# A hybrid SSD and HGRN2 encoder step: the decays of the SSD chunks computed on GpSimd, a second buffer for one tile, and one norm of the HGRN layer placed a head earlier

## The chip, the cores and the metric

The kernel runs on one core of one Trainium2 chip. The metric is the device time of one execution in microseconds (us). One profiled execution of the kernel before is at hand, with its own time and its trace, beside the times of three other runs.

## The reference, cut to what matters

The program is one inference step of a trunk of two layers, width 1024: a Mamba-2 (SSD) mixer and a SwiGLU feed-forward, then an HGRN2 mixer and another feed-forward, with 1024 prompt frames and 32 sample frames that share all weights. The change touches the scan of the SSD mixer and a norm ahead of the HGRN mixer.

```python
def step(S, inp):                       # one chunk of the SSD scan
    xc, dtc, Bc, Cc = inp
    cum = jnp.cumsum(dtc * Ag, axis=1)
    seg = cum[:, :, None] - cum[:, None, :]
    decay = jnp.where(mask, jnp.exp(jnp.where(mask, seg, 0.0)), 0.0)
    xdt = xc * dtc[..., None]
    cb = jnp.einsum('btgn,bsgn->btsg', Cc, Bc)
    y = jnp.einsum('btsg,btsgh,bsghp->btghp', cb, decay, xdt)
    y = y + jnp.einsum('btgn,bghpn->btghp', Cc, S) * jnp.exp(cum)[..., None]
    last = cum[:, -1]
    w_end = jnp.exp(last[:, None] - cum)
    S = jnp.exp(last)[..., None, None] * S + jnp.einsum('bsgh,bsghp,bsgn->bghpn', w_end, xdt, Bc)
    return S, y

def rmsnorm(x, w):
    xf = x.astype(jnp.float32)
    y = xf * lax.rsqrt(jnp.mean(xf * xf, axis=-1, keepdims=True) + NORM_EPS)
    return (y * w.astype(jnp.float32)).astype(x.dtype)
```

There are 32 SSD heads of 64 in four groups of eight; B and C (128 wide) are shared by a group. Each head has its own running sum `cum`, and so its own matrix of decays in each chunk.

## The kernel before, in words

**Tiling.** The 1056 frames lie along the free axis, in two halves of 512 and 544 columns (the 32 sample frames are the end of the second). A scheduler sorts the instructions of each engine from the order in which the code gives them, from priorities and from the buffers of each kind of tile (`BUFS`, L44); an engine then runs its list in order. Every dense projection is done as three matmuls on parts of the operands (`product`, L307 to 316: L314, L315, L316); for it each weight tile is split by ScalarE (`wh`, through the helper `act`, L98) and VectorE (`wl`, through the helper `tt`, L101). The other helpers are L104 (`stt`, VectorE), L107 (`ts`) and L110 (`dma`, issued on the queue of SyncE, SP). L331 is the matmul with ones that sums squares over the partitions.

**SSD stage.** `ssd_layer` goes through eight units, two halves by four groups. A unit has four chunks of 128 frames, and in the second half a fifth of the 32 sample frames: 36 chunks. Between the steps of a chunk stand projections as fillers for TensorE, among them z (`ssd_z`: ScalarE's tanh of the projection, then VectorE's `z` product).

For a chunk `chunk_loads` (L524) reads the running sums of the group's eight heads from DRAM, spread over all partitions, as two quads (`cumB`, kind `cb`, four buffers, so two chunks), and the factors `ec`. `ssd_chunk` (L543) then does:

- L552, the B C product on TensorE; VectorE multiplies it with the causal mask (`cbm`).
- L557, four transposes of x; VectorE makes `xdt` and `xw` of them.
- the decays: per head one ScalarE clamp of the difference, `relu(col - cumB)` on 128x128; per quad one ScalarE exp on 128x512 with scale −1, and one VectorE product with `cbm`. That is 8, 2 and 2 instructions a chunk.
- L572, the transpose of B, copied out by ScalarE (`Btok`).
- L579, C times the state; L582, the new state's product, from `xw` and `Btok`; L593, the outputs' product, 8 heads, from the products of the decays and `xdt`.

After the chunks of a group `ssd_gate` (L613 on) multiplies the output Y by z, takes its norm (squares on ScalarE, sums on VectorE, L331) and splits it. GpSimd does only small things in all this: it copies three columns at the edges of each tile of the convolution (L488 to L504), and a few powers at the start.

**HGRN stage.** `hgrn_layer` (L860) goes through sixteen units (half, head), with a list of tasks (projections) dealt out among the chunks of each. The norm of the second half is needed from unit (0,7) on. It is the last task of unit (0,6): one call of `norm` with a raised priority, which takes the squares, L331, the root (logarithm and exp on ScalarE, each with a load of its table), and writes eight pieces as a pair of tiles each (`h`, `l`).

`mixed(a, b)` deals the tasks of b evenly among those of a.

Of the kernel before, what the change touches and what calls it, by code (L numbers as in the profile page):

```python
# [11 lines left out]
AF = mybir.ActivationFunctionType  # L12
ALU = mybir.AluOpType
# [9 lines left out]
LEN = (H1, SEQ - H1 + NS)  # L23
# [14 lines left out]
C_SSDN, C_CB, C_FFN, C_HGN, C_GN, C_HG, C_LB = 0, 8, 32, 48, 56, 72, 73  # L38
# [2 lines left out]

TW = 552
FIXED = 14368
BUFS = {"x": 12, "ys": 8, "cb": 4, "xd": 2, "ec": 1, "ss": 1, "xr": 2, "n": 4, "w": 3}  # L44
WIDTH = {k: TW for k in BUFS}


@with_exitstack
def trunk_kernel(ctx, tc, x_prompt, x_sample, state_ssd, cache_conv, state_hgrn,
# [5 lines left out]
    V, A, G, PE = nc.vector, nc.scalar, nc.gpsimd, nc.tensor  # L55
# [17 lines left out]
    def slot(tag, s):  # L73
        return T(tag, s, F32R) if isinstance(tag, str) else tag
# [22 lines left out]
    def act(out, in_, f, **kw):  # L97
        A.activation(out=out, in_=in_, func=f, **kw)  # L98

    def tt(out, a, b, op, eng=None):  # L100
        (eng or V).tensor_tensor(out=out, in0=a, in1=b, op=op)  # L101
# [4 lines left out]
    def ts(out, a, s1, s2, op0, op1, eng=None):  # L106
        (eng or V).tensor_scalar(out=out, in0=a, scalar1=s1, scalar2=s2, op0=op0, op1=op1)  # L107
# [17 lines left out]
    MUL, ADD, SUB = ALU.mult, ALU.add, ALU.subtract  # L125
# [41 lines left out]
    xr = place(9)  # L167
# [170 lines left out]
    XN = [xnt[:, i] for i in range(16)]  # L338
    XN2 = ["x"] * 12 + ["cb"] * 4
# [39 lines left out]
    @lifted("norm")  # L379
    def norm(h, wc, out, tags, blocks=None, r=None):  # L380

        for (b0, bn) in blocks or ((0, LEN[h]),):
            mmb = BLK[h] if blocks is None else [(0, bn)]
            if r is None:
                r = rstd_of([acc[h][m][:, b0:b0 + bn] for m in range(KD)], mmb, 1.0 / D, bn)
            for m in range(KD):
                xf = T("n", "xf")
                stt(xf[:, :bn], acc[h][m][:, b0:b0 + bn], vc[:, wc + m:wc + m + 1], r[:, :bn], MUL, MUL)
                if m == len(out):
                    out.append((slot(tags[2 * m], "h"), slot(tags[2 * m + 1], "l")))  # L390
                xh, xl = out[m]
                act(xh[:, b0:b0 + bn], xf[:, :bn], AF.Copy)
                tt(xl[:, b0:b0 + bn], xf[:, :bn], xh[:, b0:b0 + bn].bitcast(F32), SUB)
        return out
# [8 lines left out]
    st = [place(TW) for _ in range(NG)]  # L403
# [138 lines left out]
    @lifted("chunk")  # L542
    def ssd_chunk(h, g, c, S, loads, u):  # L543
        o, n, smp = CHUNKS[h][c]
        Bt, Ct, xs, Y = u["x"][0], u["x"][1], u["x"][2:], u["Y"]
        cols, elast = dts[h]
        xo = o + (3 if smp else 0)
        Bx, Cx = Bt[:, xo:xo + n], Ct[:, xo:xo + n]
        h0 = g * 8
        cums, ec = loads  # L550
        ps = psum_sc()
        PE.matmul(ps[:n, :n], Bx, Cx, start=True, stop=True)  # L552
        cbm = small("cbm")
        tt(cbm[:n, :n], ps[:n, :n], cmask[:n, :n], MUL)
        ps = psum_sc()
        for j in range(4):
            PE.transpose(ps[:n, j * P:(j + 1) * P], xs[j][:, xo:xo + n], ident)  # L557
        x3 = ps[:n, :].rearrange("p (h q) -> p h q", q=64)
        xdt, xw = T("xd", "xdt")[:, :512], T("xd", "xw")[:, :512]
        tt(xdt[:n, :].rearrange("p (h q) -> p h q", q=64), x3,  # L560
           cols[:n, c, h0:h0 + 8].unsqueeze(2).to_broadcast([n, 8, 64]), MUL)
        tt(xw[:n, :].rearrange("p (h q) -> p h q", q=64), x3,
           cols[:n, c, 64 + h0:64 + h0 + 8].unsqueeze(2).to_broadcast([n, 8, 64]), MUL)
        for q in range(2):
            cb3 = cums[q]
            for i in range(4):
                hh = 32 + h0 + 4 * q + i
                act(cb3[:n, i, :n], cb3[:n, i, :n], AF.Relu, scale=-1.0, bias=cols[:n, c, hh:hh + 1])
            act(cb3[:n, :, :n], cb3[:n, :, :n], AF.Exp, scale=-1.0)
            tt(cb3[:n, :, :n], cb3[:n, :, :n], cbm[:n, :n].unsqueeze(1).to_broadcast([n, 4, n]), MUL)  # L570
        ps = psum_sc()
        PE.transpose(ps[:n, :P], Bx, ident)  # L572
        Btok = small("Btok")
        act(Btok[:n, :], ps[:n, :P], AF.Copy)
        if ec is not None:
            y2 = psum_sc()
            y23 = y2.rearrange("p (j t) -> p j t", t=P)
            for j in range(4):
                PE.matmul(y23[:, j, :n], S[:, j * P:(j + 1) * P], Cx, start=True, stop=True)  # L579
            tt(ec[:, :, :n], y23[:, :, :n], ec[:, :, :n], MUL)  # L580
        pp = psum_sc()
        PE.matmul(pp, Btok[:n, :], xw[:n, :], start=True, stop=True)  # L582
        if ec is None:
            V.tensor_copy(S, pp)
        else:
            S3 = S.rearrange("p (h q) -> p h q", q=64)
            tt(S3, S3, elast[:, h0:h0 + 8, c:c + 1].to_broadcast([P, 8, 64]), MUL)
            tt(S, S, pp, ADD)
        y1 = psum_sc()
        y13 = y1.rearrange("p (j t) -> p j t", t=P)  # L590
        for i in range(8):
            r = 64 * (i % 2)
            PE.matmul(y13[r:r + 64, i // 2, :n], xdt[:n, i * 64:(i + 1) * 64], cums[i // 4][:n, i % 4, :n],  # L593
                      start=True, stop=True)
        yo = Y[:, :, o:o + n]
        if ec is None:
            act(yo, y13[:, :, :n], AF.Copy)
        else:
            tt(yo, y13[:, :, :n], ec[:, :, :n], ADD)
# [260 lines left out]
    def hgrn_layer(after):  # L860
        units = [(h, e) for h in range(2) for e in range(8)]
        us = [{"S": None} for _ in units]
        for f in (hgrn_f, hgrn_q, hgrn_v):
            f(0, 0, us[0])
        for i, (h, e) in enumerate(units):
            u = us[i]
            tasks = [lambda: hgrn_g(h, e, u)]
            if e % 2 == 0 and i:
                ph, pe = units[i - 1]
                tasks += [lambda m4=m4: hgrn_out(ph, pe // 2, m4, [us[i - 2]["y"], us[i - 1]["y"]])  # L870
                          for m4 in range(2)]
            if i + 1 < len(units):
                nh, ne = units[i + 1]
                tasks += [lambda f=f: f(nh, ne, us[i + 1]) for f in (hgrn_f, hgrn_q, hgrn_v)]
            if (h, e) == (0, 6):
                tasks.append(lambda: norm(1, C_HGN, xns[1], XN2))
            if (h, e) == (1, 6):
                tasks += after[:1]
            if (h, e) == (1, 7):
                tasks += after[1:]  # L880
            u["o"] = T("ys", "ho")
            if e % 2 == 0:
                yt = sp.tile([P, 4 * TW], F32R, tag="Y", bufs=1, name=nm("hy"))[:, :4 * LEN[1]]
                yp = yt.rearrange("p (j t) -> p j t", j=4)
            u["yp"] = yp
            nch = len(CHUNKS[h])
            for c in range(nch):
                second = hgrn_chunk(h, e, c, u)
                q = -(-len(tasks) // (nch - c))
                for i2, t in enumerate(tasks[:q]):  # L890
                    if i2 == HB2:
                        second()
                    t()
                if q <= HB2:
                    second()
                tasks = tasks[q:]
            hgrn_gate(h, e, u)
        return [lambda m4=m4: hgrn_out(1, 3, m4, [us[-2]["y"], us[-1]["y"]]) for m4 in range(2)]
# [6 lines left out]
    def x_stat(h, keep):  # L905

        return rstd_of([acc[h][m][:, :LEN[h]] for m in range(KD)], BLK[h], 1.0 / D, LEN[h], keep)

    def norm_pieces(h, wc, out, blocks, r):

        def piece(m, b0, bn):
            xf = T("n", "xf")
            stt(xf[:, :bn], acc[h][m][:, b0:b0 + bn], vc[:, wc + m:wc + m + 1], r[:, b0:b0 + bn], MUL, MUL)
            if m == len(out):
                out.append((XN[2 * m], XN[2 * m + 1]))
            xh, xl = out[m]
            act(xh[:, b0:b0 + bn], xf[:, :bn], AF.Copy)
            tt(xl[:, b0:b0 + bn], xf[:, :bn], xh[:, b0:b0 + bn].bitcast(F32), SUB)
        return [lambda m=m, b=b: piece(m, *b) for b in blocks for m in range(KD)]
# [209 lines left out]
    def mixed(a, b):  # L1129

        out, k = [], 0
        for i, x in enumerate(a):
            out.append(x)
            while k < len(b) and k * len(a) < (i + 1) * len(b):
                out.append(b[k])
                k += 1
        return out + b[k:]
# [163 lines left out]
```

## Time and profile before

| what | before |
|---|---|
| three runs | 2904.81, 2904.77, 2899.86 us, median 2904.77 |
| the profiled execution | 2906.18 us; its span 2904.4 us, mean granted TensorE clock 0.996 |
| idle time of TensorE in the span | 55.6 us |
| instructions in the span | 49072 |
| clamps on ScalarE, exps on ScalarE, products on VectorE | 288, 72 and 72 instructions; 93.4, 42.3 and 44.5 us |

Times in rows are us from the span's start; a timeline row has start, duration, engine, line, operation, the tile written and the tiles read, how many instructions are drawn together, and in brackets the idle time before them with what ended it. A row of groups has the busy time, the mean of one in ns, and the idle time ahead of them. A windows row has the busy time of each engine and its count, then the granted clock of TensorE (1.00 is full), the DMA share and GB/s. A wait for several things is put down to the one that the profile saw last. L98, L101, L104, L107 and L110 are lines of helpers, so operations are told apart by their tiles.

### The profile page before, as it was taken

To read this page: it belongs to the slowest core of one execution; us is meant where nothing else is said; L and a number is where in the kernel's file an instruction comes from. 1 tells how busy PE (TensorE), PEld (TensorE's weight loads), DVE (VectorE), ACT (ScalarE), POOL (GpSimd) and SP (SyncE) were. 2 spreads that over 40 slices of the span, in tenths; PEclk is the share of its full clock that TensorE was granted. 3 is DMA by queue.
4 is the path that set the end of the run, shared out by engine and by line. 5 is a ranking of instruction groups with operands and counts; after the bars stand their busy time and mean duration, and the time that the engine had idled before them with its cause. 6 is when DMAs were issued, how large, how long until landed. Compare 5 with 4: busy or idle time off the path is not lost. (4 is left out here: it accounts for less than half of the span.)

```text
span 2904.4 us, 49072 instructions
## 1 busy us (share of the span) xinstructions
PE 2848.8 (98%) x19711; PEld 2619.9 (90%) x19711; DVE 2152.7 (74%) x3744; ACT 1559.5 (54%) x2922; POOL 46.4 (2%) x156
## 2 busy tenths in 40 slices
PE   8999999999999999999999999999999999999998
PEld 7777788999988999999999888899988999999998
DVE  6777787777787977887777455655568877887777
ACT  6645645554653754456544655655554644554445
POOL 0000000000000000000000000000000000000000
PEclk9999999999999999999999999999999999999999
DMA  5443434344332333323333222222222332333223
GB/s 151 115 111 92 110 82 120 109 114 108 107 90 88 102 111 100 102 80 95 109 95 105 81 82 73 60 79 77 74 84 81 119 100 88 120 94 94 90 88 111
DMA packets 401247, 282.61 MB, mean 97 GB/s; under 512 B 22633, under 2 KB 388730, under 8 KB 401018
## 3 DMA queue, kind: packets, MB, share of 16 engines
q1 hardware_dynamic: 401018, 279.47, 33.2%
q8 instruction: 154, 2.52, 0.3%
q14 instruction: 75, 0.61, 0.1%
HBM read 271.61 MB, written 7.82 MB: 96 GB/s over the span
## 5 line engine op out<-in xcount | busy, mean ns | idle before, releaser
L98 ACT ACTIVATE wh<-raw 128x512 fp32r<-128x512 f32 (+1 forms) x688 | 557.3, 818 | 541.8 <-PE mm L315 419.5
L314 PE MATMUL mm<-xn,wh 128*128 128x272 f32 (+2 forms) x1552 | 524.8, 338 | 0.3 <-ACT wh L98 0.3
L315 PE MATMUL mm<-xn,wh 128*128 128x272 f32 (+2 forms) x1552 | 519.1, 335 | 3.8 <-issue 3.8
L316 PE MATMUL mm<-xn,wl 128*128 128x272 f32 (+2 forms) x1552 | 518.5, 334 | 3.2 <-DVE wl L101 3.2
L101 DVE TENSOR_TENSOR wl<-raw,wh 128x1024 fp32r<-128x1024 f32 x308 | 375.9, 1222 | 83.7 <-ACT wh L98 63.5
L101 DVE TENSOR_TENSOR fixed<-mm,fixed 128x272 f32<-128x272 f32 (+1 forms) x512 | 262.9, 525 | 192.7 <-PE mm L316 191.1
L314 PE MATMUL mm<-fh,wh 128*128 128x272 f32 (+1 forms) x1056 | 341.7, 325 | 1.1 <-DVE fixed L101 0.8
L315 PE MATMUL mm<-fl,wh 128*128 128x272 f32 (+1 forms) x1056 | 341.9, 324 | 0.7 <-DVE fl L101 0.7
L316 PE MATMUL mm<-fh,wl 128*128 128x272 f32 (+1 forms) x1056 | 341.7, 324 | 0.0
L316 PEld LDWEIGHTS mm<-xn,wl 128*128 128x128 f32 x1552 | 293.0, 189 | 37.3 <-issue 6.0
L314 PEld LDWEIGHTS mm<-xn,wh 128*128 128x128 f32 x1552 | 293.0, 189 | 29.5 <-issue 2.6
L315 PEld LDWEIGHTS mm<-xn,wh 128*128 128x128 f32 x1552 | 293.0, 189 | 27.1 <-issue 0.8
L101 DVE TENSOR_TENSOR wh<-raw,wh 128x512 fp32r<-128x512 f32 x380 | 257.1, 688 | 38.5 <-ACT wh L98 35.2
L989 PE MATMUL mm<-th,wh 128*128 128x272 f32 (+1 forms) x912 | 260.4, 286 | 0.1
L990 PE MATMUL mm<-tl,wh 128*128 128x272 f32 (+1 forms) x912 | 259.7, 285 | 0.0
L991 PE MATMUL mm<-th,wh 128*128 128x272 f32 (+1 forms) x912 | 259.6, 285 | 0.0
L314 PEld LDWEIGHTS mm<-fh,wh 128*128 128x128 f32 x1056 | 198.4, 188 | 17.4 <-DVE fixed L101 1.7
L315 PEld LDWEIGHTS mm<-fl,wh 128*128 128x128 f32 x1056 | 198.7, 188 | 16.3 <-DVE fl L101 1.8
L316 PEld LDWEIGHTS mm<-fh,wl 128*128 128x128 f32 x1056 | 198.7, 188 | 15.3
L989 PE MATMUL sc<-xn,wh 128*128 128x272 f32 (+1 forms) x608 | 173.2, 285 | 0.5 <-ACT wh L98 0.5
L989 PEld LDWEIGHTS mm<-th,wh 128*128 128x128 f32 x912 | 171.8, 188 | 1.9 <-ACT s L98 1.2
L990 PE MATMUL sc<-xn,wh 128*128 128x272 f32 (+1 forms) x608 | 173.2, 285 | 0.0
(251 smaller groups left out, 6637.0 us busy)
## 6 DMA issues: line engine op xcount, KB each, us to landing
raw<-in_ffn_w_down_dram SPq DMA_DIRECT2D x90, 512.0 KB, 3.5
raw<-in_ffn_w_gate_dram SPq DMA_DIRECT2D x88, 512.0 KB, 3.8
raw<-in_ffn_w_up_dram SPq DMA_DIRECT2D x88, 512.0 KB, 4.6
raw<-in_ssd_in_w_dram SPq DMA_DIRECT2D x80, 512.0 KB, 4.0
raw<-in_hgrn_in_w_dram SPq DMA_DIRECT2D x64, 512.0 KB, 4.2
cumB<-cumd SPq DMA_DIRECT2D x64, 256.0 KB, 4.5
raw<-in_ssd_out_w_dram SPq DMA_DIRECT2D x32, 512.0 KB, 3.5
raw<-in_hgrn_out_w_dram SPq DMA_DIRECT2D x16, 512.0 KB, 3.3
```

Source lines behind the costliest of these rows:

```text
L98: A.activation(out=out, in_=in_, func=f, **kw)
L101: (eng or V).tensor_tensor(out=out, in0=a, in1=b, op=op)
L314: PE.matmul(ps[:, :bn], a, mh, start=(k == 0), stop=False)
L315: PE.matmul(ps[:, :bn], a, ml, start=False, stop=False)
L316: PE.matmul(ps[:, :bn], b, mh, start=False, stop=(k == n - 1))
L989: PE.matmul(ps[:, :n], a, mh, start=(k == 0 and not more), stop=False, skip_group_check=True)
L990: PE.matmul(ps[:, :n], a, ml, start=False, stop=False, skip_group_check=True)
L991: PE.matmul(ps[:, :n], b, mh, start=False, stop=(k == 3), skip_group_check=True)
```

## The change

Three things change.

1. In `ssd_chunk` the clamp of the differences goes from ScalarE to GpSimd, as `min(cumB - col, 0)` in place of `relu(col - cumB)`; the exp on ScalarE loses its scale; the product with `cbm` goes from VectorE to GpSimd. The counts stay: 8, 2 and 2 a chunk.
2. `ec` has two buffers instead of one.
3. In the HGRN stage the statistic of the second half's norm (squares, L331, root) becomes the last task of unit (0,5), and its eight pieces become tasks dealt among the projections of unit (0,6), without the raised priority. `norm_pieces` gets a parameter for the kinds of tiles that it writes.

```diff
-BUFS = {"x": 12, "ys": 8, "cb": 4, "xd": 2, "ec": 1, "ss": 1, "xr": 2, "n": 4, "w": 3}
+BUFS = {"x": 12, "ys": 8, "cb": 4, "xd": 2, "ec": 2, "ss": 1, "xr": 2, "n": 4, "w": 3}
...
                 hh = 32 + h0 + 4 * q + i
-                act(cb3[:n, i, :n], cb3[:n, i, :n], AF.Relu, scale=-1.0, bias=cols[:n, c, hh:hh + 1])
-            act(cb3[:n, :, :n], cb3[:n, :, :n], AF.Exp, scale=-1.0)
-            tt(cb3[:n, :, :n], cb3[:n, :, :n], cbm[:n, :n].unsqueeze(1).to_broadcast([n, 4, n]), MUL)
+                ts(cb3[:n, i, :n], cb3[:n, i, :n], cols[:n, c, hh:hh + 1], 0.0, SUB, ALU.min, G)
+            act(cb3[:n, :, :n], cb3[:n, :, :n], AF.Exp)
+            tt(cb3[:n, :, :n], cb3[:n, :, :n], cbm[:n, :n].unsqueeze(1).to_broadcast([n, 4, n]), MUL, G)
...
+            if (h, e) == (0, 5):
+                tasks.append(lambda: r.append(x_stat(1, st[2])))
             if (h, e) == (0, 6):
-                tasks.append(lambda: norm(1, C_HGN, xns[1], XN2))
+                tasks = mixed(tasks, norm_pieces(1, C_HGN, xns[1], ((0, LEN[1]),), r[0], XN2))
...
-    def norm_pieces(h, wc, out, blocks, r):
+    def norm_pieces(h, wc, out, blocks, r, tags=XN):
...
-                out.append((XN[2 * m], XN[2 * m + 1]))
+                out.append((slot(tags[2 * m], "h"), slot(tags[2 * m + 1], "l")))
```

The scheduler places the instructions anew. On ScalarE, in group 2 of the first half, this stands in a row before; the quads 2550 and 2552 belong to the third chunk of the group, 2638 and 2640 to the fourth, and `fixed<-sc` is `Btok` of the second chunk (2581) and of the third (2669):

```order
L98 ACTIVATE fixed<-sc_2581 128x128
L98 ACTIVATE cumB_2552<-cumB_2552,fixed 128x128 x3
L98 ACTIVATE wh_2775<-raw_2773 128x1024
L98 ACTIVATE cumB_2552<-cumB_2552 128x512
L98 ACTIVATE cumB_2638<-cumB_2638,fixed 128x128 x4
L98 ACTIVATE cumB_2640<-cumB_2640,fixed 128x128
L98 ACTIVATE cumB_2638<-cumB_2638 128x512
L98 ACTIVATE z_2610<-mm_2611 128x512
L98 ACTIVATE fixed<-sc_2669 128x128
L98 ACTIVATE cumB_2640<-cumB_2640,fixed 128x128 x3
L98 ACTIVATE wh_2853<-raw_2851 128x1024
L98 ACTIVATE cumB_2640<-cumB_2640 128x512
```

The same place on ScalarE now:

```order
L98 ACTIVATE wh_2775<-raw_2773 128x1024
L98 ACTIVATE z_2522<-mm_2523 128x512
L98 ACTIVATE fixed<-sc_2581 128x128
L98 ACTIVATE cumB_2550<-cumB_2550 128x512
L98 ACTIVATE cumB_2552<-cumB_2552 128x512
L98 ACTIVATE cumB_2638<-cumB_2638 128x512
L98 ACTIVATE cumB_2640<-cumB_2640 128x512
L98 ACTIVATE wh_2853<-raw_2851 128x1024
L98 ACTIVATE z_2610<-mm_2611 128x512
L98 ACTIVATE fixed<-sc_2669 128x128
```

Before, the clamps of one quad, one clamp of the next and an exp stood ahead of z and `Btok` of the third chunk; now both exps of the fourth chunk's quads and `wh` do. In the second chunk z and `Btok` stand ahead of all exps.

On GpSimd the same chunks stand so now, with nothing of the kind there before (2469 and 2471 are the second chunk):

```order
L107 TENSOR_SCALAR cumB_2550<-cumB_2550,fixed 128x128 x4
L107 TENSOR_SCALAR cumB_2552<-cumB_2552,fixed 128x128 x3
L101 TENSOR_TENSOR cumB_2469<-cumB_2469,fixed 128x512
L101 TENSOR_TENSOR cumB_2471<-cumB_2471,fixed 128x512
L107 TENSOR_SCALAR cumB_2552<-cumB_2552,fixed 128x128
L107 TENSOR_SCALAR cumB_2638<-cumB_2638,fixed 128x128 x4
L107 TENSOR_SCALAR cumB_2640<-cumB_2640,fixed 128x128 x4
L101 TENSOR_TENSOR cumB_2550<-cumB_2550,fixed 128x512
L101 TENSOR_TENSOR cumB_2552<-cumB_2552,fixed 128x512
```

The clamps of a chunk stand ahead of the products of the chunk before it.

On TensorE, in the HGRN stage, this stood before at the norm of the second half, at the end of unit (0,6); the first two rows are the norm's statistic, `h` are its pieces:

```order
L331 MATMUL sc_19067<-sq_19043,fixed 128x272
L331 MATMUL sc_19070<-sq_19043,fixed 128x272
L821 MATMUL sc_19122<-hkv_19041 128x128
L314 MATMUL mm_19157<-xn,wh_19153 128x512
L315 MATMUL mm_19157<-xn,wh_19153 128x512
L316 MATMUL mm_19157<-xn,wl_19154 128x512
L823 MATMUL sc_19124<-fixed,hkv_19041 128x128
L825 MATMUL sc_19124<-hq_18655,fixed 128x128
L314 MATMUL mm_19157<-xn,wh_19153 128x512
L315 MATMUL mm_19157<-xn,wh_19153 128x512
L316 MATMUL mm_19157<-xn,wl_19154 128x512
L314 MATMUL mm_19205<-h_19076,wh_19201 128x272
```

Now the statistic stands at the end of unit (0,5), followed by other work, and nothing of `h` comes until unit (0,7). A little behind it stand the gate of unit (0,5) and the first chunk of (0,6) (sc_18780 is the gate's sum of squares, `hkv` the state's addend, `hy` the operand of the output projection):

```order
L314 MATMUL mm_18856<-hy_18228,wh_18852 128x512
L315 MATMUL mm_18856<-hy_18228,wh_18852 128x512
L331 MATMUL sc_18780<-sq_18777,fixed 128x512
L806 MATMUL sc_18790<-hq_18639,hk_18615 128x128
L810 MATMUL sc_18793<-fixed,hk_18615 128x128
L811 MATMUL sc_18793<-fixed,hv_18690 128x128
L316 MATMUL mm_18856<-hy_18228,wl_18853 128x512
L314 MATMUL mm_18864<-hy_18228,wh_18852 128x512
L315 MATMUL mm_18864<-hy_18228,wh_18852 128x512
L316 MATMUL mm_18864<-hy_18228,wl_18853 128x512
L821 MATMUL sc_18832<-hkv_18796 128x128
```

Between the head's output product (L811) and the next state step (L821) four fillers stand here.

More of the change, by code (lines that the diff above doesn't have):

```diff
@@ L862, in hgrn_layer @@
         us = [{"S": None} for _ in units]
+        r = []
         for f in (hgrn_f, hgrn_q, hgrn_v):
```

## The prediction

> **What bounds the kernel now.** I read the page's busy shares first, then the chain, then the waits view, then the timeline of TensorE through the SSD stage, and at last the other engines round its waits.
>
> ```profile
> PE 2848.8 (98%) x19711; PEld 2619.9 (90%) x19711; DVE 2152.7 (74%) x3744; ACT 1559.5 (54%) x2922; POOL 46.4 (2%) x156
> ```
>
> TensorE is busy for 2848.8 of 2904.4 us, so all its gaps together are 55.6 us. The change removes no matmul: it can only gain from gaps, or open new ones. The windows view says where they are.
>
> ```profile
> 100.00:460.00 360.00, 341.89 (x1862) 275.23 (x1861) 284.00 (x432) 201.70 (x387) 20.68 (x59) 1.00 0.39 104
> 480.00:860.00 380.00, 379.01 (x2998) 352.88 (x2997) 297.14 (x487) 204.61 (x444) 17.98 (x70) 1.00 0.39 106
> ```
>
> In these rows the sums are PE, PEld, DVE, ACT, POOL, then the granted clock. The SSD stage of the first half (100 to 460) loses 18.1 us of TensorE, that of the second half (480 to 860) 1.0 us. The waits view names the losses that the change touches (us in total, times, longest):
>
> ```profile
> ACT cumB L98 <- DMA cumB<-cumd: 51.5, 21, 8.6
> PE sc L582 <- ACT wh L98: 5.0, 4, 1.7
> PE sc L582 <- DVE xw L101: 3.9, 4, 1.4
> ```
>
> L582 is the state product of a chunk, 8.9 us in all. The 51.5 us in the first row are ScalarE's waits for the broadcast of the running sums, and they are the root: what is queued on ScalarE behind the clamp waits for that DMA. One chunk of the first half (the third of its group) shows the chain; the rows are of SP, ScalarE, VectorE and TensorE:
>
> ```profile
> 189.30 0.91 SPq L110 DMA_DIRECT2D cumB<-cumd  x2
> ```
> ```profile
> 193.52 1.70 ACT L98 ACTIVATE cumB<-cumB,fixed 128x128 f32<-128x128 f32 x5 [5.51 <-DMA cumB<-cumd]
> 195.13 0.61 ACT L98 ACTIVATE cumB<-cumB 128x512 f32<-128x512 f32 x1
> 195.65 0.58 ACT L98 ACTIVATE z<-mm 128x512 f32<-128x512 f32 x1
> ...
> 197.16 1.05 ACT L98 ACTIVATE wh<-raw 128x1024 fp32r<-128x1024 f32 x1
> ```
> ```profile
> 196.26 0.69 DVE L104 SCALAR_TENSOR_TENSOR z<-z,mm 128x512 f32<-128x512 f32 x1 [1.36 <-ACT z L98]
> ...
> 197.46 0.68 DVE L101 TENSOR_TENSOR xw<-sc,fixed 128x512 f32<-128x512 f32 x1
> ```
> ```profile
> 187.58 1.10 PE L582 MATMUL sc<-xw,fixed 128*128 128x512 f32 x2 [1.72 <-ACT wh L98]
> 188.60 0.66 PE L593 MATMUL sc<-cumB,xdt 128*64 128x128 f32 x8
> 198.29 1.10 PE L582 MATMUL sc<-xw,fixed 128*128 128x512 f32 x2 [1.16 <-ACT wh L98]
> ```
>
> Call T the start of L593 of the chunk before (188.60), which frees the buffers for the next load. The DMA goes out at T+0.7 and lands at T+4.9; four clamps of the first quad of heads and one of the second follow, then exp, then z at T+7.05. VectorE's z product waits for that, xw stands behind it and ends at 198.14, and L582 starts 0.15 later. So the wait that is put down to ACT wh is really for xw. Without its wait L582 would have started at 198.29 − 1.16 = T+8.53.
>
> **The change, term by term.** *Prices on GpSimd.* The trace has no 128x128 subtract-and-clamp and no 128x512 product there.
>
> ```profile
> masks.py:199 POOL TENSOR_SCALAR_AFFINE_SELECT fixed<-fixed 128x128 f32<-128x128 f32 x1 | 0.3, 292 | 0.0
> L101 POOL TENSOR_TENSOR fixed<-fixed 128x2 f32<-128x2 f32 x2 | 1.4, 706 | 12.3 <-DVE fixed L107 12.3
> ```
> ```profile
> L101 DVE TENSOR_TENSOR cumB<-cumB,fixed 128x512 f32<-128x512 f32 (+1 forms) x72 | 44.5, 641 | 0.5
> L98 ACT ACTIVATE cumB<-cumB,fixed 128x128 f32<-128x128 f32 (+1 forms) x288 | 93.4, 383 | 59.2 <-DMA cumB<-cumd 51.5 <-PE mm L315 6.9 <-DVE cumB L101 0.3
> ```
>
> A clamp I take at 0.29 us, the one tile of that size (upper bound 0.71, the power on a tiny tile, whose operation is dearer). The product, four times the elements, I take at 4 × 0.29 = 1.17 (lower bound 0.64, VectorE's mean for it; upper bound 1.9, since a GpSimd instruction can be held up, see the rivals). Per chunk GpSimd gets 8 × 0.29 + 2 × 1.17 = 4.7 us of a period of 10.7 us. ScalarE loses 93.4 us and VectorE 44.5 us in all, both off the path except where something queues behind them.
>
> *Third and fourth chunk of groups 1 and 2, first half.* In the new order of ScalarE both exps of the next chunk stand ahead of wh, z and the transposed B. The second quad's load lands at about T+6.2 (it is issued half a microsecond behind the first; bounds 5.3 and 7.0). Then four clamps on GpSimd 1.16, a handover 0.1, exp 0.6, wh 1.05 (0.95 from start to start): z starts at T+9.1 where it was T+7.05, z's product follows at T+9.7, xw is done at T+10.9, and L582 starts at T+11.0. That is 2.45 us of waiting. These are the waits now:
>
> ```profile
> 209.08 1.10 PE L582 MATMUL sc<-xw,fixed 128*128 128x512 f32 x2 [1.29 <-DVE xw L101]
> 286.56 0.67 PE L582 MATMUL sc<-xw,fixed 128*128 128x512 f32 x1 [1.27 <-ACT wh L98]
> 296.89 1.10 PE L582 MATMUL sc<-xw,fixed 128*128 128x512 f32 x2 [0.81 <-ACT wh L98]
> 307.85 1.10 PE L582 MATMUL sc<-xw,fixed 128*128 128x512 f32 x2 [1.41 <-DVE xw L101]
> ```
>
> The four (1.16, 1.29, 0.81, 1.41) have the mean 1.17; so +1.28 each, **+5.1 us** (bounds: +1.5 with the early landing, +8.3 with the late one).
>
> *Second chunk of groups 1 and 2.* There the exps come behind z and the transposed B, so the waits of 1.72 and 1.27 go: **−3.0**. What is late next is L593, which needs both products: clamps of the next chunk until T+7.4, two products until T+9.7, wanted at T+9.56. It is nearly even; 0 to +1.2 each stays in the range.
>
> *Group 0.* Its first half has no wh in that place; its two L582 waits go.
>
> ```profile
> 96.61 1.10 PE L582 MATMUL sc<-xw,fixed 128*128 128x512 f32 x2 [0.63 <-DVE xw L101]
> 114.73 1.13 PE L582 MATMUL sc<-xw,fixed 128*128 128x512 f32 x2 [0.97 <-ACT fixed L98]
> ```
>
> That is **−1.6**. *Gates* (the ones-matmul of each group's norm, which waits for squares): ScalarE is freer, but exps that wait for GpSimd now stand ahead of the squares; **0 ± 2**. *Second half.* A state product is never waited for there:
>
> ```profile
> 502.06 0.38 PE L552 MATMUL sc<-ca,ca 128*128 128x128 f32 x2
> ...
> 505.51 1.09 PE L593 MATMUL sc<-cumB,xdt 128*64 128x128 f32 x16
> ```
>
> From the B C product to L593 there are 3.45 us, and mask (0.3, plus 0.2 of handover) with two products at 1.17 takes 2.84: **0**, until a product costs over 1.47. *ec in two buffers* takes its loads on SP off the wait for the output of the chunk before; behind them on SP is only the next chunk's load, which waits for its own buffer: **0** (0 to −1).
>
> *The clock.* Waits on TensorE can cost twice. The windows below have the granted clock third from the end:
>
> ```profile
> 128.00:132.00 4.00, 3.94 (x11) 2.52 (x12) 2.44 (x4) 3.97 (x7) 0.53 (x2) 0.57 0.39 132
> 184.00:188.00 4.00, 2.28 (x10) 1.46 (x9) 2.46 (x5) 3.89 (x9) 0.00 (x0) 1.00 0.11 33
> 1844.00:1848.00 4.00, 2.94 (x12) 2.46 (x13) 4.00 (x6) 2.43 (x4) 0.00 (x0) 0.65 0.00 0
> 1848.00:1852.00 4.00, 4.00 (x20) 4.00 (x20) 4.00 (x8) 1.84 (x3) 0.00 (x0) 0.50 0.45 135
> ```
> ```profile
> 128.06 0.58 PE L316 MATMUL mm<-xn,wl 128*128 128x512 f32 x1 [1.98 <-DVE wl L101]
> 1844.44 0.77 PE L314 MATMUL mm<-h,wh 128*128 128x272 f32 x4 [3.15 <-ACT h L98]
> ```
>
> After a wait of 1.98 us the clock was 0.57 for 4 us, a loss of 1.7; after 3.15 us it was 0.65 and 0.50, a loss of 3.4; after 1.72 us it stayed at 1.00. Four new waits of 2.45 lie above; at 1.7 each and a little over even odds, **+4** (0 to +7). [...]
>
> *HGRN.* The norm of the second half leaves the end of unit (0,6), where h is late and 3.15 us pass at one place; its statistic runs a unit earlier and its eight pieces lie among the projections. The wait goes, with the 3.4 of clock behind it, of which I count 3.0: −6.2. New places are the ones-matmul of the head's own gate and the next state product, which now stand behind a table load and an exp on ScalarE:
>
> ```profile
> 1840.93 1.28 ACT L98 ACT_TABLE_LOAD   x1
> 1842.22 0.66 ACT L98 ACTIVATE rstd<-rstd 128x544 f32<-128x544 f32 x1
> ```
>
> Each costs between 0 (fillers cover it) and 1.94 (nothing does); half of it twice is +1.9. HGRN gives **−4.3** (−7 to −2.3).
>
> **Sum:** 5.1 − 3.0 − 1.6 + 0 + 0 + 4 − 4.3 = +0.2 us on the profiled 2906.18 (span 2904.4 plus 1.8 around it), 2906.4. The median of the three runs, 2904.77, is 1.4 below the profiled time, so **2905.0 us**: no change.
>
> **Rivals.** *A, the exps come in time (faster).* If the second load lands at T+5.3 and the clock never falls, the four chunks cost 1.5 instead of 9.1: −7.6; with a gate gain of −1 the time is about 2896. For it: GpSimd begins to clamp the moment a load lands, with nothing of another kind queued ahead of it in these chunks. Against it: z's start depends on exactly this load, and it was seen late.
>
> *B, the product is dear (slower).* Place: L593 in every chunk. From 1.47 us a product it stalls the second half, 2 × (price − 1.47) for each of its 16 full chunks; at 1.9 that is 13.8 us, and the second chunks of the first half add 2 × 0.73 each, 2.9: +17, 2922. For it: this copy of three columns began beside a run of VectorE work on operands from SBUF (the first of it below) and ended only after it:
>
> ```profile
> 756.58 2.60 POOL L503 COPY fixed<-pre 128x3 f32<-128x3 f32 x1 [11.18 <-ACT pre L98]
> ```
> ```profile
> 756.57 0.72 DVE L101 TENSOR_TENSOR yl<-Y,yh 128x544 fp32r<-128x544 f32 x1
> ```
>
> Against it: ahead of L593 VectorE works mostly on operands from PSUM (xdt, xw, z), and the product has 3.45 us there.
>
> *C, the lock falls on VectorE.* The same row lets me think that the two engines exclude each other on such operands, so GpSimd may hold VectorE instead: 4.7 us a chunk. VectorE would go from 284 to about 284 − 20 + 16 × 4.7 = 339 of 360 us in the first half: near full, and every late wl stops a filler. At 0.7 us for some 20 chunks: +14, 2919. [...]
>
> *D, HGRN's gain is eaten* by the new waits at full price: +2 on the forecast, 2907, still within 0.2%.
>
> **Numbers.** A measurement of this kernel can tell about 0.2%, 5.8 us: same is 2899.0 to 2910.6. Forecast with its own spread (2899 to 2910.6) 0.35, A 0.32, B 0.14, C 0.13, D 0.06. Faster 0.32, same 0.41, slower 0.27. The range takes in A with HGRN at its lower bound and the gates at theirs (2896 − 2.7 − 1 = 2892), and the middle of B and C (2920).
>
> **What would show it.** Right: in the profile after, L582 waits of 2 to 3 us in the third and fourth chunks of groups 1 and 2 and none in the second; no wait at h in HGRN; GpSimd rows near 0.29 and 1.17 us; second half of SSD still within 1 to 2 us of gaps. Wrong: waits of L593 for GpSimd (B), waits of L316 for wl in the SSD stage and VectorE's two-input rows longer than before (C), or z's row at T+7 as now (A).

## The result and the profile after

| | us, median (lowest to highest) | runs |
|---|---|---|
| before | 2902.28 (2898.69 to 2904.81) | 5 |
| changed | 2980.24 (2977.18 to 2985.36) | 5 |

The ratio is 1.0271, with a 95% interval from 1.0255 to 1.0286: the changed kernel is 78 us slower. The span of its profiled execution is 2978.5 us, 74.1 more than before. The page's first part, in the same order as before:

```profile
PE 2873.4 (96%) x19711; PEld 2634.8 (88%) x19711; DVE 2130.9 (72%) x3672; ACT 1477.9 (50%) x2634; POOL 366.0 (12%) x516
```

The matmuls are the same 19711. TensorE is busy 24.6 us longer (2873.4 against 2848.8), and idle for 105.1 us of the span, 49.5 more than the 55.6 of before. So a third of the loss is not in gaps but in matmuls at a lower clock (0.984 in the mean of the span, against 0.996). The same two stretches as before in the windows view (sums of PE, PEld, DVE, ACT, POOL, then the granted clock) show where:

```profile
100.00:460.00 360.00, 304.46 (x1416) 233.94 (x1414) 220.94 (x319) 137.52 (x219) 131.33 (x174) 0.92 0.31 83
480.00:860.00 380.00, 372.41 (x2901) 350.01 (x2900) 283.40 (x432) 175.83 (x322) 175.08 (x260) 1.00 0.40 107
```

The first half of the SSD stage has gaps of 55.5 us in 360, at a clock of 0.92; before it had 18.1 at 1.00. The stages shift against each other, so I line the kernels up by one matmul: the first ones-matmul (L331) of the last gate of each half starts at 422.69 and 867.12 us before, and at 485.05 and 942.90 now. The first half is 62.4 us late, the second adds 13.4, and what follows gives 1.7 back. Who is waited for now, in the waits view:

```profile
ACT cumB L98 <- POOL cumB L107: 193.0, 61, 12.5
...
PE sc L331 <- DVE sq L101: 18.1, 4, 7.7
...
PE sc L582 <- DVE xw L101: 18.0, 8, 5.1
PE sc L593 <- POOL cumB L101: 13.9, 6, 7.1
...
PE sc L579 <- ACT fixed L98: 12.7, 2, 6.4
```

The first row is the new one: ScalarE waits 193.0 us for GpSimd's clamps, where before it waited 51.5 us for their DMA. The groups of GpSimd say why:

```profile
L107 POOL TENSOR_SCALAR cumB<-cumB,fixed 128x128 f32<-128x128 f32 x256 | 218.6, 871 | 65.1 <-DMA cumB<-cumd 55.8 <-PE sc L579 8.2 <-PE sc L593 0.7
L101 POOL TENSOR_TENSOR cumB<-cumB,fixed 128x512 f32<-128x512 f32 x64 | 84.6, 1342 | 168.3 <-DVE fixed L101 168.3
```

A clamp took 0.871 us in the mean where I had 0.29; a product 1.342 where I had 1.17. The chunk of the prediction's example (third of group 1), now, in the timelines of GpSimd, ScalarE, VectorE and TensorE:

```profile
202.90 5.54 POOL L107 TENSOR_SCALAR cumB<-cumB,fixed 128x128 f32<-128x128 f32 x8 [2.76 <-DMA cumB<-cumd]
208.40 2.53 POOL L101 TENSOR_TENSOR cumB<-cumB,fixed 128x512 f32<-128x512 f32 x2
```
```profile
205.71 0.63 ACT L98 ACTIVATE cumB<-cumB 128x512 f32<-128x512 f32 x1 [4.91 <-POOL cumB L107]
208.47 0.63 ACT L98 ACTIVATE cumB<-cumB 128x512 f32<-128x512 f32 x1 [2.12 <-POOL cumB L107]
209.01 1.04 ACT L98 ACTIVATE wh<-raw 128x1024 fp32r<-128x1024 f32 x1
209.95 0.58 ACT L98 ACTIVATE z<-mm 128x512 f32<-128x512 f32 x1
```
```profile
210.56 0.69 DVE L104 SCALAR_TENSOR_TENSOR z<-z,mm 128x512 f32<-128x512 f32 x1 [2.15 <-ACT z L98]
211.17 0.69 DVE L101 TENSOR_TENSOR xw<-sc,fixed 128x512 f32<-128x512 f32 x1
```
```profile
198.27 2.35 PE L593 MATMUL sc<-cumB,xdt 128*64 128x128 f32 x16 [2.86 <-POOL cumB L101]
212.00 1.10 PE L582 MATMUL sc<-xw,fixed 128*128 128x512 f32 x2 [1.92 <-DVE xw L101]
226.61 2.04 PE L582 MATMUL sc<-xw,fixed 128*128 128x512 f32 x2 [5.07 <-DVE xw L101]
```

The eight clamps run back to back for 5.54 us, 0.69 each, with VectorE idle for 4.6 us of it. Behind them on ScalarE stand exp, wh and z in turn, then VectorE's z product and xw, and L582 starts at T+13.7 (T is 198.27). The links are those of the prediction; each starts when the one ahead of it ends. TensorE waited for only 1.92 us of that because its own work up to there was slower: at a clock of 0.50 from 200 to 204 it reached L582 at T+11.8, where before it was ready at T+8.53.

### The profile page after: what moved, and what is told of

The parts are those of the page before. It is cut to its first block, busy times and chain, and to the rows that moved or that the text cites. A ratio compares the mean times of both kernels' runs of the same rounds, so it can differ in the third digit from the quotient of the medians.

```text
span 2978.5 us, 49214 instructions
## 1 busy us (share of the span) xinstructions
PE 2873.4 (96%) x19711; PEld 2634.8 (88%) x19711; DVE 2130.9 (72%) x3672; ACT 1477.9 (50%) x2634; POOL 366.0 (12%) x516
## 4 chain that ended last, share of the span: by engine, by line
PE 84%; POOL 5%; DVE 4%; DMA 3%; ACT 3%; issue 2%; SPq 0%; DVEq 0%; POOLq 0%; ACTq 0%
PE mm L314 17%; PE mm L316 17%; PE mm L315 17%; PE mm L994 5%; PE mm L992 5%; PE mm L993 5%; POOL cumB L107 4%; PE sc L994 4%; PE sc L992 4%; PE sc L993 4%; DMA cumB<-cumd 1%; PE sc L331 1%; PE sc L582 1%; DMA raw<-in_ssd_in_w_dram 1%; PE sc L593 1%
## 5 line engine op out<-in xcount | busy, mean ns | idle before, releaser
L101 DVE TENSOR_TENSOR wl<-raw,wh 128x1024 fp32r<-128x1024 f32 x308 | 379.2, 1232 | 85.7 <-ACT wh L98 63.3
L314 PEld LDWEIGHTS mm<-xn,wh 128*128 128x128 f32 x1552 | 294.6, 190 | 30.6 <-issue 2.1
L994 PE MATMUL mm<-th,wh 128*128 128x272 f32 (+1 forms) x912 | 259.6, 285 | 0.0
L107 POOL TENSOR_SCALAR cumB<-cumB,fixed 128x128 f32<-128x128 f32 (+1 forms) x288 | 234.8, 833 | 67.6 <-DMA cumB<-cumd 58.2
```

The source lines that it names most:

```text
L314: PE.matmul(ps[:, :bn], a, mh, start=(k == 0), stop=False)
L994: PE.matmul(ps[:, :n], b, mh, start=False, stop=(k == 3), skip_group_check=True)
```

## The experiments

Each time stands against runs of the kernel before on the same chip. Line numbers of the kernels with a few more lines are shifted (L587 is the state product L582 there, L598 is L593).

**1 and 2: the two small parts alone.** `e1_hgrn_only` is the kernel before with the HGRN part of the diff; `e2_ec_only` changes one number:

```diff
-"ec": 1
+"ec": 2
```

> Only the HGRN norm a head sooner; the SSD stage as before, ec in one buffer. Lined up by their matmuls, the two traces differ by +75.1 us ahead of the HGRN layer and by +73.2 us behind it, so the norm alone should give about -2 us (2900). If the whole loss lay in this part: about +78.

> Only the second buffer for ec. The prediction had 0 (0 to -1). The scheduler moves some rows, so -3 to +3 us; more than +6 would make the second buffer a cause of its own.

Measured: 2900.76 us against 2901.74, ratio 0.9994 (0.9985 to 1.0003), and 2902.62 us, 1.0001 (0.9992 to 1.0010). Neither can be told from no change, and neither carries the loss.

**3 and 4: the two halves of the move to GpSimd.** Each is made in the kernel before, by itself:

```diff
 # e3_clamps_only
-act(cb3[:n, i, :n], cb3[:n, i, :n], AF.Relu, scale=-1.0, bias=cols[:n, c, hh:hh + 1])
+ts(cb3[:n, i, :n], cb3[:n, i, :n], cols[:n, c, hh:hh + 1], 0.0, SUB, ALU.min, G)
-act(cb3[:n, :, :n], cb3[:n, :, :n], AF.Exp, scale=-1.0)
+act(cb3[:n, :, :n], cb3[:n, :, :n], AF.Exp)
 # e4_products_only
-tt(cb3[:n, :, :n], cb3[:n, :, :n], cbm[:n, :n].unsqueeze(1).to_broadcast([n, 4, n]), MUL)
+tt(cb3[:n, :, :n], cb3[:n, :, :n], cbm[:n, :n].unsqueeze(1).to_broadcast([n, 4, n]), MUL, G)
```

> Only the clamps on GpSimd; products stay on VectorE, ec in one buffer, no HGRN part. Clamp theory (eight clamps of 0.69 us in a row stand ahead of exp and z on ScalarE, so the state product is late and the clock falls): +50 to +85 us. Product theory (two products of 1.3 us and their collisions with VectorE are what is late): within 10 us of before.

> Only the products on GpSimd; clamps stay on ScalarE, ec in one buffer, no HGRN part. Clamp theory: 0 to +12 us, from L593 waiting for the second product in the first half. Product theory: +40 us or more, L593 waiting for GpSimd in most chunks.

Measured: clamps 2982.49 us, 1.0277 (1.0261 to 1.0293), 81 us over; products 2901.81 us, 1.0001 (0.9992 to 1.0010). The clamps alone are the whole loss, and the product theory falls.

**5: what a clamp pays for.** The changed kernel with six forms of instruction in place of the eight clamps, one of them (two of the eight) the change's own.

> The changed kernel with the eight clamps of a chunk replaced by seven forms of GpSimd instruction on the same 128x128 tiles, each on a line of its own: subtract and min with a column (as in the change, heads 0 and 5), with two constants (1 and 6), min with a column alone (2), min with a column and a product with 1 (3), a copy (4), min with a constant alone (7). The decays are not those of the reference. If the clamp's 0.69 us is the price of two operations or of the column, some form takes 0.3 us (the estimate of 0.29 came from an instruction without a column); if it is the price of the elements, all take about 0.7.

One execution took 2963.65 us. GpSimd's timeline of one chunk, with VectorE nearly idle beside it:

```profile
218.78 0.73 POOL L570 TENSOR_SCALAR cumB<-cumB,fixed 128x128 f32<-128x128 f32 x1 [6.73 <-DMA cumB<-cumd]
219.47 0.64 POOL L572 TENSOR_SCALAR cumB<-cumB 128x128 f32<-128x128 f32 x1
220.09 0.61 POOL L574 TENSOR_SCALAR cumB<-cumB,fixed 128x128 f32<-128x128 f32 x1
220.68 0.72 POOL L576 TENSOR_SCALAR cumB<-cumB,fixed 128x128 f32<-128x128 f32 x1
221.35 0.29 POOL L580 COPY cumB<-cumB 128x128 f32<-128x128 f32 x1
...
222.92 0.54 POOL L578 TENSOR_SCALAR cumB<-cumB 128x128 f32<-128x128 f32 x1
```

L570 is the change's form (column, two operations), L572 has constants, L574 and L578 one operation (column, constant), L576 another second operation, L580 is a copy. All the arithmetic forms take 0.54 to 0.73 us: the column costs about 0.08, the second operation about 0.1. Only the copy takes 0.29, the price that I had read off a select by index (292 ns).

**6 and 7: the same instructions at a lower price.** In `e3_clamps_only` each clamp is narrowed to its first 8, or 32, columns; decays in the other columns are not clamped. The order on the engines is close to that of `e3_clamps_only`, not the same.

```diff
-ts(cb3[:n, i, :n], cb3[:n, i, :n], cols[:n, c, hh:hh + 1], 0.0, SUB, ALU.min, G)
+ts(cb3[:n, i, :min(n, 8)], cb3[:n, i, :min(n, 8)], cols[:n, c, hh:hh + 1], 0.0, SUB, ALU.min, G)
```

> As e3_clamps_only, but each clamp works on the first 8 of 128 columns (the others are not clamped), so the same instructions in nearly the same order, at a lower price of about 0.35 us each. Price theory: eight of them take 2.8 us, near the 2.3 that was predicted, and the loss falls from 80 us to between 0 and 15. Order theory (the exps of the next chunk ahead of z cost it whatever the clamp's price): still over 40.

> As e6_narrow8 with 32 of 128 columns, about 0.42 us a clamp. Price theory: between e6_narrow8 and e3_clamps_only, some 10 to 30 us over before. Order theory: still over 40.

Measured: 2934.05 us, 1.0104 (1.0090 to 1.0117), and 2941.51 us, 1.0131 (1.0117 to 1.0144), against 2903.49. Four narrow clamps of GpSimd, in the third chunk of group 1 of `e6_narrow8`:

```profile
209.86 1.20 POOL L107 TENSOR_SCALAR cumB<-cumB,fixed 128x8 f32<-128x8 f32 x4 [8.84 <-DMA cumB<-cumd]
```

At 0.30 us a clamp undisturbed, the price that I had put down (0.52 in the mean of the kernel, with the clamps that something held up), the loss is still 30.6 us, at 32 columns 38, and at 0.69 (0.91 in the mean) 81. Both runs lie between the two theories (0 to 15 and 10 to 30 for the price, over 40 for the order). The price carries 50 us. The other 30 come near my own price, but they are not shown to be the order's alone, since held-up clamps still cost more than 0.30. In the profile of `e6_narrow8` they are 15.7 us of gaps (71.3 in all against 55.6) and 11.5 us of longer busy time, at a lower clock (0.990 against 0.996).

**8: the clamps on VectorE.** As `e3_clamps_only`, without the last argument `G`.

> The clamps on VectorE instead of GpSimd, products on VectorE, ec in one buffer, no HGRN part; the order on ScalarE again has the exps ahead of z. At 0.2 to 0.3 us a clamp VectorE gets 2 us more a chunk, where ScalarE loses 2.6. Price theory: -3 to +8 us. Order theory: over +40.

Measured: 2921.66 us, 1.0062 (1.0048 to 1.0076), 18 us over: outside both expectations.

```profile
L107 DVE TENSOR_SCALAR cumB<-cumB,fixed 128x128 f32<-128x128 f32 x256 | 57.6, 280 | 20.4 <-DMA cumB<-cumd 19.0 <-PE sc L579 1.3
```
```profile
PE mm L316 <- DVE wl L101: 15.3, 3, 9.3
```

The clamp costs 0.28 us here, and much of the loss sits in another queue. The two long waits for VectorE's weights (wl) are 4.49 us at 129.09 and 9.30 at 446.33. But ahead of the second no clamp runs on VectorE from 420 on: it works on the gate, on dt and on the convolution, and the split starts seven instructions behind the scan of dt (L446), where in the kernel before one started right behind that scan. So the list of VectorE came out in another order, and why it did is not shown. The clamps' own waits for loads (19.0 us on VectorE) show only in small waits of TensorE: L582 waits for xw 6.3 us in all, the longest 1.8. So this run has an order of its own and does not tell the two theories apart.

**9 and 10: full price, no queue.** `e9_hold4` is `e3_clamps_only` with a tie: a tiny ScalarE instruction writes a zero column behind Btok, and the exps of the next chunk take it as their bias. `e10_hold6` has six buffers of kind `cb` beside that.

```diff
 act(Btok[:n, :], ps[:n, :P], AF.Copy)
+at["hold"] = (at["hold"] + 1) % 4
+act(hold[:n, at["hold"]:at["hold"] + 1], Btok[:n, 0:1], AF.Copy, scale=0.0)
...
-act(cb3[:n, :, :n], cb3[:n, :, :n], AF.Exp)
+act(cb3[:n, :, :n], cb3[:n, :, :n], AF.Exp, bias=hold[:n, at["hold"]:at["hold"] + 1])
```

> As e3_clamps_only, with the full clamps on GpSimd at 0.69 us, but the exps of a chunk are tied behind the transposed B of the chunk before (their bias is a zero column that ScalarE writes right behind it, one tiny instruction a chunk), so z and the transposed B no longer queue behind clamps. Queue theory (the loss is ScalarE's list standing still at exps that wait for GpSimd): from +80 to +5 to +25 us, since wh still stands behind the exps. Throughput theory (GpSimd or VectorE is simply too busy): over +50 as before.

> As e9_hold4 with six buffers for the running sums instead of four, so loads and clamps of a chunk run one chunk earlier and the exps find them done. Queue theory: -5 to +5 us against before, at the same 0.69 us a clamp. Throughput theory: over +50.

Measured: 2905.78 us, 1.0019 (1.0009 to 1.0029), and 2906.77 us, 1.0020 (1.0011 to 1.0030), against 2900.46. GpSimd and ScalarE in the third chunk of group 1 of `e9_hold4`:

```profile
200.26 6.33 POOL L107 TENSOR_SCALAR cumB<-cumB,fixed 128x128 f32<-128x128 f32 x8 [1.75 <-DMA cumB<-cumd]
```
```profile
201.66 0.58 ACT L98 ACTIVATE z<-mm 128x512 f32<-128x512 f32 x1
202.13 0.27 ACT L98 ACTIVATE fixed<-sc 128x128 f32<-128x128 f32 x1
202.44 0.20 ACT L98 ACTIVATE fixed<-fixed 128x1 f32<-128x1 f32 x1
203.54 0.73 ACT L98 ACTIVATE cumB<-cumB,fixed 128x512 f32<-128x512 f32 x1 [0.91 <-POOL cumB L107]
206.63 0.72 ACT L98 ACTIVATE cumB<-cumB,fixed 128x512 f32<-128x512 f32 x1 [2.36 <-POOL cumB L107]
```

The clamps are as dear as ever, and ScalarE still waits for them, but now behind z and the transposed B. Of 81 us 5 are left, so most of the loss was in what stood behind the exps on ScalarE, not in how busy GpSimd is: it is busy for longer here (323 us against 290 in `e3_clamps_only`). The sixth buffer gains nothing (6.3 us over, just above what was expected), though ScalarE's waits for the clamps fall from 59.4 to 11.5 us: how early the clamps are done is not what matters once nothing urgent stands behind them.

**11: the whole change with the tie.**

> The whole change (clamps and products on GpSimd, two buffers for ec, the norm a head sooner) with the tie and the six buffers of e10_hold6. Queue theory: the L582 waits of before go too, -3 to -15 us. Throughput theory: over +50.

Measured: 2925.42 us, 1.0084 (1.0069 to 1.0099): the expectation of a gain was wrong. The waits view, and GpSimd and TensorE in the fourth chunk of group 1:

```profile
PE sc L598 <- POOL cumB L101: 21.3, 14, 5.1
```
```profile
213.13 6.70 POOL L107 TENSOR_SCALAR cumB<-cumB,fixed 128x128 f32<-128x128 f32 x8 [6.14 <-DMA cumB<-cumd]
219.80 2.48 POOL L101 TENSOR_TENSOR cumB<-cumB,fixed 128x512 f32<-128x512 f32 x2
```
```profile
221.11 2.35 PE L598 MATMUL sc<-cumB,xdt 128*64 128x128 f32 x16 [5.13 <-POOL cumB L101]
```

With ScalarE's queue mended, GpSimd's own queue is next: the products of a chunk stand behind the eight clamps of the following one, and those wait for a load. This is the place of rival B, at the clamp's price. Clamps and products on the same engine hurt where the products alone (`e4_products_only`) did not.

**12: the tie in the kernel before.** The clamps stay on ScalarE and take their scale from a column of −1 written behind Btok; the HGRN part is in.

```diff
-act(cb3[:n, i, :n], cb3[:n, i, :n], AF.Relu, scale=-1.0, bias=cols[:n, c, hh:hh + 1])
+act(cb3[:n, i, :n], cb3[:n, i, :n], AF.Relu, scale=hold[:n, at["hold"]:at["hold"] + 1], bias=cols[:n, c, hh:hh + 1])
```

> A version that might beat both: the clamps stay on ScalarE and the products on VectorE, but the clamps of a chunk are tied behind the transposed B of the chunk before, as the exps were in e9_hold4 (their scale is a column of -1 that ScalarE writes behind it); with the HGRN part of e1_hgrn_only. If ScalarE's queue is what delays L582 in the kernel before too, its 8.9 us of L582 waits go and the HGRN norm gives 1 more: -5 to -10 us (2891 to 2896). If the waits only move to L593 or to the weights' split behind the exps: within 3 us of before.

Measured: 2890.45 us against 2903.15, ratio 0.9956 (0.9942 to 0.9969): 12.7 us faster than before, the fastest kernel of this study, and a little more than expected. ScalarE round the same chunk, and the one wait of the state product that is left:

```profile
197.76 0.58 ACT L98 ACTIVATE z<-mm 128x512 f32<-128x512 f32 x1
198.23 0.27 ACT L98 ACTIVATE fixed<-sc 128x128 f32<-128x128 f32 x1
198.53 0.20 ACT L98 ACTIVATE fixed<-fixed 128x1 f32<-128x1 f32 x1
198.77 2.04 ACT L98 ACTIVATE cumB<-cumB,fixed 128x128 f32<-128x128 f32 x5
```
```profile
PE sc L587 <- ACT cumB L98: 1.1, 1, 1.1
```

z and the transposed B go first, the clamps follow without a gap, since their load landed meanwhile, and in the whole kernel ScalarE's waits for that load fall from 51.5 to 1.6 us. The waits of the state product fall from 9.9 us (the prediction's 8.9 and 1.0 for ScalarE's `fixed`) to 1.1. A clamp is dearer here (a median of 0.48 us against 0.39, with its scale from a column), and the kernel is faster all the same. The tie thus gains some 12 us without GpSimd too (the HGRN part alone, `e1_hgrn_only`, was 1.0 us faster, which can't be told from nothing). Against this kernel, rather than against before, the tied clamps on GpSimd of `e9_hold4` still cost about 17 us (5.3 + 12.7 − 1), as far as a tie of the exps and one of the clamps compare.

## Why the prediction was wrong, point by point

- **The clamp at 0.29 us: wrong, and this is the step that failed.** It is 0.69 undisturbed. I took the row of the same shape (a select by index, 292 ns), not of the same kind. The upper bound of 0.71 stood in the text, but I never put it through the sum: the rivals let only the product grow dear. With 0.69 the second quad no longer waits for its own landing but for the first quad's clamps: landing at T+4.9, eight clamps to T+10.4, L582 at about T+14, a wait of 5.4 instead of 2.45 (seen: 1.92 to 5.07). For the four chunks of the sum that is 12 us more, not 78. The rest came at places behind the same exps that my sum put at nothing or left out. Against before, TensorE's waits in the SSD stage grew by 15.0 us at the gates (L331), 13.9 at L593, 12.9 at L582 and 12.3 at L579, and its busy time by 24.6. Most of this came with the price: with the clamps alone on GpSimd, L582 grew by 19.4 us and L331 by 14.7 at 0.69 a clamp (`e3_clamps_only`), by 4.3 and 2.5 at 0.30 (`e6_narrow8`). Only busy time was still 11.5 us longer there, where my clock term was 4.
- **The product at 1.17: right in size** (1.25 undisturbed, 1.34 in the mean), and nothing alone (`e4_products_only`).
- **Third and fourth chunks of groups 1 and 2: right place and chain**, size as above. **The second chunk**: its L582 waits went, and L593 became late for GpSimd as I had feared (2.86 at 198.27).
- **Group 0, −1.6: wrong sign.** Its L582 waits are 3.19 and 1.41 us now (at 105.75 and 113.72).
- **Group 3 of the first half: no term in my sum.** There L579 waits 6.22 us at 435.15 for ScalarE's copy of the transposed B, behind two exps, and L593 7.07 us at 461.82 for its products, which stand on GpSimd behind the clamps of the next chunk.
- **Gates, 0 ± 2: wrong.** L331 waits for 17.8 us at three gates of the SSD stage where it was 2.8. I had named the cause, exps that wait for GpSimd ahead of the squares, and given it no price. The longest, at the gate of group 0 (ScalarE, then TensorE):

```profile
126.95 0.63 ACT L98 ACTIVATE cumB<-cumB 128x512 f32<-128x512 f32 x1 [4.18 <-POOL cumB L107]
129.79 0.63 ACT L98 ACTIVATE cumB<-cumB 128x512 f32<-128x512 f32 x1 [2.21 <-POOL pre L488]
130.32 1.13 ACT L98 ACTIVATE sq<-Y 128x512 f32<-128x512 f32 x2
```
```profile
134.96 2.07 PE L331 MATMUL sc<-sq,fixed 128*128 128x512 f32 x2 [7.68 <-DVE sq L101]
```

The eight clamps end at 129.75, just ahead of the second exp. Near my own clamp price, in `e6_narrow8`, the gates were nearly right (5.3 us against 2.8), but the SSD part as a whole costs 30.6, not the 4.5 of my terms (5.1 − 3.0 − 1.6 + 4). Its order differs a little from the changed kernel's, and its products are on VectorE, so 30.6 is not exactly what the change would have lost.

- **The clock, +4: right in kind, a sixth of the size.** Busy time grew by 24.6 us.
- **Second half, 0: wrong by 13.4 us.** Half of it is one wait, 6.44 us of L579 at the first chunk of the last group (887.58), until ScalarE has copied the transposed B: again ScalarE's list. State products, which I had never waited for there, wait 3.6 us in all. The product's 3.45 us of slack held.
- **ec, 0: right** (`e2_ec_only`).
- **HGRN, −4.3: right sign, too large.** From one gate of HGRN to a later one the two traces show −1.8:

```profile
1769.71 1.12 PE L331 MATMUL sc<-sq,fixed 128*128 128x512 f32 x2
1990.83 1.08 PE L331 MATMUL sc<-sq,fixed 128*128 128x272 f32 x4
```
```profile
1844.81 1.12 PE L331 MATMUL sc<-sq,fixed 128*128 128x512 f32 x2
2064.09 1.08 PE L331 MATMUL sc<-sq,fixed 128*128 128x272 f32 x4
```

The first pair is of before (221.12 us apart), the second of the changed kernel (219.28). The wait for h is gone, and the new waits are longer than my 1.9: two of 1.0 and 0.9 for the squares at L331, 1.0 at L810, 0.7 at L821, 3.6 in all.

- **The rivals.** A did not come. B had one of the places (L593 waits 13.9 us for GpSimd), with the wrong instruction as cause. C is there but rare. In `e5_prices` a product and a weight's split met, GpSimd and then VectorE:

```profile
198.48 3.63 POOL L101 TENSOR_TENSOR cumB<-cumB,fixed 128x512 f32<-128x512 f32 x2
```
```profile
198.70 2.29 DVE L101 TENSOR_TENSOR wl<-raw,wh 128x1024 fp32r<-128x1024 f32 x1
```

Two products alone take 2.5, the split alone 1.22: each lost about 1.1, so here both engines were held up, where C had the loss on VectorE. Beside VectorE's work on operands from PSUM (xdt, z and xw, 195.61 to 197.50 in the same run) GpSimd's clamps and copy kept their prices (0.62 to 0.73 and 0.30), as the argument against B had it. But the mean of all 308 splits went only from 1222 to 1232 ns in the changed kernel. GpSimd's clamps lost more (0.87 us in the mean against 0.69 undisturbed); no run isolates what held them up.

What stays open: where the 5 us that `e9_hold4` still loses against before lie, and how much of the 30 us of `e6_narrow8` is due to the order and how much to clamps that were held up.

## What to carry to other kernels

ScalarE's list was a queue here: two exps of 0.63 us, which waited 4.91 and 2.12 us for their clamps (205.71 and 208.47), delayed wh, z and the transposed B behind them. Before moving work to a slower engine, ask what stands behind its consumer on a third engine, and whether a tie can put the urgent work first; here the tie with the clamps left on ScalarE was faster than every other placement that was run. When a price is bounded from both sides, put both bounds through the whole chain, not only through the term that they stand in.

## What the runs showed of the hardware

- GpSimd's arithmetic on 128x128 floats took 0.54 to 0.73 us in `e5_prices`, where a copy took 0.29. For the change's clamp VectorE took 0.28 in `e8_clamps_dve`, and GpSimd 0.69 undisturbed in the changed kernel: a factor of 2.5. For the product of two tiles it was 1.25 on GpSimd undisturbed against 0.69 on VectorE before: a factor of 1.8.
- The granted clock did not follow the length of a wait alone. In the changed kernel it stayed at 1.00 after the 1.92 us at 212.00, but was 0.57 in the 4 us after a wait of 1.26 us at 1334.50 (L994); in the profile before it was 0.57 after 1.98 us. Round the 5.07 us at 226.61 it was 0.68 and then 0.50:

```profile
212.00:216.00 4.00, 4.00 (x26) 2.73 (x27) 3.39 (x5) 0.00 (x0) 0.00 (x0) 1.00 0.19 51
224.00:228.00 4.00, 1.39 (x2) 0.50 (x2) 2.82 (x5) 1.31 (x3) 1.52 (x2) 0.68 0.00 0
228.00:232.00 4.00, 4.00 (x21) 2.80 (x21) 2.75 (x4) 0.00 (x0) 0.00 (x0) 0.50 0.17 48
```
